# A feed-forward in two passes through DRAM, with seven block products in place of eight

## The chip, the cores and the metric

One core of one Trainium2 chip. The metric is the device time of the program in microseconds; several executions are measured, and the median is given. TensorE is PE in the profile, VectorE DVE, ScalarE ACT, GpSimd POOL, and SyncE SP; all DMAs of this kernel are issued on SP.

## The reference

Two layers of a diffusion backbone over 1280 tokens (1024 latent tokens and 256 context tokens, width 1024). Each layer has a mixer (attention, a recurrent branch, a gated MLP) and then a feed-forward with 4096 features; both end in a normalised residual sum:

```python
def _layer(x, mod, lp, ctx):
    sh1, sc1, g1, sh2, sc2, g2 = jnp.split(mod, 6, axis=-1)
    out, k, v, s = _mixer(x * (1 + sc1) + sh1, lp, ctx)
    x = _layernorm(ALPHA * x + g1 * out, lp['ln1_g'], lp['ln1_b'])
    hff = x * (1 + sc2) + sh2
    f = jnp.square(jax.nn.relu(hff @ lp['w_ff1'] + lp['b_ff1'])) @ lp['w_ff2'] + lp['b_ff2']
    x = _layernorm(ALPHA * x + g2 * f, lp['ln2_g'], lp['ln2_b'])
    return x, k, v, s
```

The change is in the line of `f`. `mod`, the modulation, is a product of a condition vector with a 1024 x 6144 matrix for each layer.

## The kernel before

**Arithmetic.** Every fp32 operand of a product is split into `hi` (12 significant bits, ACT copies it) and `lo = src - hi` (`split`, line 159; POOL or DVE subtracts, line 166). A product is then three matmuls into the same PSUM bank, hi·hi, lo·hi and hi·lo (`mm3`, lines 168 to 172). A bank holds 128 x 512, and eight banks are free in the feed-forward.

**Feed-forward.** `ff` (line 1412 on) runs over 16 chunks of 256 features. `ff1` makes a chunk's hidden features, feature-major, in three token groups A, B (512 latent tokens each) and C (256 context tokens): 8 x 3 matmuls to a bank, ACT relu (line 1386) and square (1387), and DVE squares once more in place and subtracts for the low part (1388, 1389). `ff2_mm` then makes, for each of ten blocks of 128 tokens (`BLOCKS`), 2 x 2 x 3 matmuls of 512 columns into two banks, and DVE adds them to the running sum in SBUF, `acc[t]`:

```python
nc.vector.tensor_tensor(acc[t][:, ns], b[n], (bf if c == 0 else acc[t])[:, ns], ALU.add)   # line 1446
```

So each chunk's hidden features are used at once and never leave SBUF. Weights come in pieces of 128 x 1024 (512 KB); `ahead` keeps two pieces split (`whi`, `wlo`) and four on their way (`stg`).

**The end of a layer.** Chunks 14 and 15 have their first products one after the other; then the final stage (lines 1475 to 1500) does both second products of a block in one go (24 matmuls), and the block's gate, residual and normalisation follow on DVE, with `ln_stats` (its Newton steps are lines 184 and 188). In layer 1 the last scaling is shared by POOL (line 1488, 1489) and DVE. Ahead of it, `conv` (lines 1420 to 1429) turns `acc` into `acc * gate + x` on POOL, in the background, from chunk 13's first block on.

**Order of the work.** The program is written out in one order per engine. Background streams (`add_bg`, `tick`) hand out pieces of work at a rate beside the main loops: in layer 0's feed-forward, `ada_bg` makes the remaining modulation on DVE (lines 462 to 500, rate `ABR = 0.36`), 14 halves of 16 operations. Buffers are pools: U with 30 buffers of 4 KB a partition for the whole program, X with 20 in this phase.

Of the kernel before, what the change touches and what calls it, by code (L numbers as in the profile page):

```python
# [8 lines left out]
F32 = mybir.dt.float32  # L9
# [29 lines left out]
NX = (20, 20)  # L39
# [12 lines left out]
ABR = 0.36  # L52
# [24 lines left out]
class Kern:  # L77
# [16 lines left out]
    def x_open(self, bufs):  # L94
        """the part of SBUF, and PSUM, that each phase cuts to its own sizes"""
# [62 lines left out]
    def split(self, hi, lo, src, hi_eng="act", lo_eng="pool"):  # L158
        """hi = src to 12 significant bits, lo = the rest, both exact."""
# [31 lines left out]
    def gelu2(self, dst, b):  # L191
        """dst (SBUF) = 2 gelu(b), the tanh form, of b in PSUM"""
# [23 lines left out]
    def pieces_init(self):  # L216
# [8 lines left out]
        for l in range(DEPTH):  # L225
# [26 lines left out]
    def pal(self, p, stg=False):  # L252
# [37 lines left out]
    def ahead(self, key, n_split, n_dma):  # L290
        """pieces up to n past key's are split, and n_dma past it on their way"""
        i = self.pidx[key]
        self.p_emit_split(i + 1 + n_split)
        self.p_emit_dma(i + 1 + n_dma)

# [1 line left out]
    def ada_load(self, l, part, c0, k0, alloc, s):  # L297
        """rows k0 * 128 ... and 256 columns of the modulation's weights"""
# [1307 lines left out]
```

## Time and profile before

| | |
|---|---|
| median of three runs | 3286.34 us |
| lowest, highest | 3280.35, 3291.84 us |
| span of the profiled execution | 3283.4 us |
| PE busy, matmuls and transposes | 3063.7 us, 16,368 |
| DVE busy | 2272.3 us |
| ACT busy | 1264.4 us |
| POOL busy | 1073.3 us |
| moved by DMA | 215.37 MB |

The profiled execution is one of its own; the page gives its span, from the first instruction to the last, and no other time of it. Its span lies 2.9 us below the median and within the runs shown. A matmul row's duration is longer than its share of the time, since matmuls are pipelined: the distance between two starts is what counts.

### The profile page before, as it was taken

How to read it: one execution, taken by the hardware profiler on the slowest of the kernel's cores; microseconds unless marked ns; L12 is line 12 of the kernel's file. 1: busy time of each engine (PE TensorE's matmuls, PEld its weight loads, DVE VectorE, ACT ScalarE, POOL GpSimd, SP SyncE). 2: the span in 40 equal slices, each digit the busy share in tenths (PEclk: the TensorE clock that was granted, in tenths of full speed). 3: DMA queues.
4: the chain of work that ended last, by engine and by line, in shares of the span. 5: the costliest groups of instructions: out<-in, count | busy, mean ns of one | idle time of the engine just before them, and what ended most of it. 6: DMA issues, size and time to landing. Idle time of an engine off the chain costs nothing. (4 is left out here: it accounts for less than half of the span.)

```text
span 3283.4 us, 42645 instructions
## 1 busy us (share of the span) xinstructions
PE 3063.7 (93%) x16368; PEld 2586.6 (79%) x16368; DVE 2272.3 (69%) x4688; ACT 1264.4 (39%) x2098; POOL 1073.3 (33%) x606
## 2 busy tenths in 40 slices
PE   7888999999999999999988899997899999999994
PEld 5676789777888888888877778985688888888883
DVE  8879999686767757664747999968743434343469
ACT  5444688543212121222466457872412121212121
POOL 4222245442222222226333224466411111111364
PEclk9999999999999999999999999998899999999997
DMA  6321000232222222212221100021300111111221
GB/s 223 125 83 43 15 1 14 91 109 96 91 65 90 90 78 78 90 65 90 79 76 46 55 15 1 8 103 71 116 29 36 40 38 39 39 39 39 71 90 58
DMA packets 105084, 215.37 MB, mean 66 GB/s; under 512 B 16248, under 2 KB 49800, under 8 KB 104880
## 3 DMA queue, kind: packets, MB, share of 16 engines
q1 hardware_dynamic: 104880, 212.65, 18.8%
q8 instruction: 128, 2.10, 0.3%
q14 instruction: 76, 0.62, 0.1%
HBM read 185.82 MB, written 26.81 MB: 65 GB/s over the span
## 5 line engine op out<-in xcount | busy, mean ns | idle before, releaser
L166 POOL TENSOR_TENSOR wlo<-stg,whi 128x1024 fp32r<-128x1024 f32 (+2 forms) x196 | 432.6, 2224 | 1156.3 <-ACT whi L162 967.6
L170 PE MATMUL ps<-hh,whi 128*128 128x512 f32 (+1 forms) x1808 | 647.6, 358 | 20.4 <-ACT hh L561 10.2
L172 PE MATMUL ps<-hh,wlo 128*128 128x512 f32 (+1 forms) x1808 | 645.8, 357 | 5.4 <-POOL wlo L166 5.4
L171 PE MATMUL ps<-hl,whi 128*128 128x512 f32 (+1 forms) x1808 | 643.2, 356 | 5.4 <-POOL hl L383 2.2
L1386 ACT ACTIVATE relu<-ps,pfm 128x512 f32<-128x512 f32 (+1 forms) x192 | 118.1, 616 | 1164.6 <-PE ps L172 1104.5
L1388 DVE TENSOR_TENSOR relu<-relu 128x512 f32<-128x512 f32 (+1 forms) x192 | 164.0, 855 | 489.0 <-ACT midh L1387 419.4
L1446 DVE TENSOR_TENSOR acc<-ps,acc 128x512 f32<-128x512 f32 x520 | 347.5, 687 | 207.3 <-PE ps L172 207.1
L170 PE MATMUL ps<-whi,midh 128*128 128x512 f32 x1024 | 401.1, 392 | 0.0
L172 PE MATMUL ps<-whi,midl 128*128 128x512 f32 x1024 | 400.6, 391 | 0.0
L171 PE MATMUL ps<-wlo,midh 128*128 128x512 f32 x1024 | 400.4, 391 | 0.0
L170 PEld LDWEIGHTS ps<-hh,whi 128*128 128x128 f32 x1808 | 342.8, 190 | 71.2 <-ACT hh L561 10.6
L171 PEld LDWEIGHTS ps<-hl,whi 128*128 128x128 f32 x1808 | 342.2, 189 | 61.8 <-POOL hl L383 3.9
L172 PEld LDWEIGHTS ps<-hh,wlo 128*128 128x128 f32 x1808 | 342.0, 189 | 58.8 <-POOL wlo L166 6.3
L166 POOL TENSOR_TENSOR pt<-ptf,pt 128x512 fp32r<-128x512 f32 x128 | 166.7, 1303 | 240.2 <-DVE pt L164 224.2
L1144 DVE TENSOR_SCALAR_CACHE_REDUCE S<-sc 128x512 f32<-128x512 f32 (+1 forms) x416 | 224.4, 581 | 11.2 <-PE pT L1155 9.9
L172 PEld LDWEIGHTS ps<-whi,midl 128*128 128x128 f32 x1024 | 192.9, 188 | 41.1
L170 PEld LDWEIGHTS ps<-whi,midh 128*128 128x128 f32 x1024 | 193.2, 189 | 39.7
L171 PEld LDWEIGHTS ps<-wlo,midh 128*128 128x128 f32 x1024 | 193.2, 189 | 39.5
L1147 ACT ACTIVATE S<-S,anm 128x1280 f32<-128x1280 f32 (+1 forms) x160 | 191.1, 1195 | 36.8 <-DVE anm L1146 34.5
L1155 PE MATMUL pT<-ident,S 128*128 128x128 f32 x1344 | 201.8, 273 | 2.0 <-DVE pt L1164 1.4
L162 ACT CAST whi<-stg 128x1024 fp32r<-128x1024 f32 (+2 forms) x204 | 178.2, 910 | 56.8 <-DMA stg<-in_w_ff 28.3
L1180 PE MATMUL o<-pt,vt 128*128 128x256 f32 x1024 | 190.9, 302 | 9.8 <-POOL pt L166 8.0
(318 smaller groups left out, 6133.8 us busy)
## 6 DMA issues: line engine op xcount, KB each, us to landing
stg<-in_w_ff SPq DMA_DIRECT2D x128, 512.0 KB
aslab<-in_w_ada SPq DMA_DIRECT2D x56, 512.0 KB
rx<-rx SPq DMA_DIRECT2D x40, 512.0 KB
stg<-in_w_in SPq DMA_DIRECT2D x28, 512.0 KB
araw<-in_w_ada SPq DMA_DIRECT2D x48, 256.0 KB
wada<-in_w_ada SPq DMA_DIRECT2D x16, 512.0 KB
stg<-in_w_out SPq DMA_DIRECT2D x16, 512.0 KB
yf<-ydr SPq DMA_DIRECT2D x20, 256.0 KB
```

Source lines behind the costliest of these rows:

```text
L162: nc.scalar.copy(hi, src)
L166: e.tensor_tensor(lo, src, hi.bitcast(F32), ALU.subtract)
L170: mm(out, lh, rh, start=start, stop=False)
L171: mm(out, lh, rl, start=False, stop=False)
L172: mm(out, ll, rh, start=False, stop=stop)
L1144: nc.vector.tensor_scalar(S[:, c0:c0 + n], b[:, :n], 1.0, -3.0e38, ALU.mult, ALU.max, accum_out=u["m"][:, hh, i:i + 1])
L1147: nc.scalar.activation(S[:, :c0], S[:, :c0], AF.Exp, bias=u["nm"][:, hh:hh + 1], accum_out=u["d"]["den"][:, ci % 2, hh:hh + 1])
L1155: nc.tensor.transpose(b[:, c, hh, :], u["S"][hh][:, (2 * j + c) * P:(2 * j + c + 1) * P], self.ident)
L1180: nc.tensor.matmul(o, v, pt[:, hl, c, :], start=j == 0 and c == 0 and hl == 0, stop=j == last and c == 1 and hl == 1)
L1386: nc.scalar.activation(f[:, :n], b[:, :n], AF.Relu, bias=pf[:, C_BF1 + 2 * c + m:C_BF1 + 2 * c + m + 1])
L1388: nc.vector.tensor_tensor(f[:, :n], f[:, :n], f[:, :n], ALU.mult)
L1446: nc.vector.tensor_tensor(acc[t][:, ns], b[n], (bf if c == 0 else acc[t])[:, ns], ALU.add)
```

## The change

The feed-forward makes two passes. **Pass 1** runs all 16 first products. Each feature half `m` goes to a tile `f[m]` of [128, 2, 640], in which the 1280 tokens are two halves of 640 (512 latent and 128 context tokens); ACT takes relu and square. For chunks 0 to 11 the 2 x 2 arrangement (feature half by token half) is turned into the seven left operands of a Strassen product in Winograd's form: three are the tiles themselves, four are sums on DVE, and all seven are stored to DRAM (`mc`). Chunks 12 to 15 are stored plain (`mr`). **Pass 2** (`seven`) goes through six groups `q` of two chunks. For each of seven products it loads M (`mf`, 640 KB), splits it on ACT and DVE (`mh`, `ml`), makes the weights' operand by differences on POOL (four of the seven), splits it (`wh`, `wl`), and multiplies: five token blocks of 128 x two chunks x three matmuls of 512 columns. Each result goes to one of the accumulators X1, X2, Y, Z. In the last group these are joined to the ten blocks' sums. Chunks 12 and 13 then follow as before from `mr` (`mid_load`), `conv` is added behind the first block of chunk 13 with all ten blocks, and the final stage with chunks 14 and 15 is as before. The background modulation moves from X to U and its rate from 0.36 to 0.62. X has 14 buffers and a ring of eight tiles of 5 KB (`m`), which also takes weights in the out-projection.

```diff
-NX = (20, 20)
+NX = 14
+NM = 8
+NQ = 6
-ABR = 0.36
+ABR = 0.62
...
 def ff1
+        f = [self.mt([P, 2, 640], s="f") for _ in range(2)]
...
+                nc.scalar.activation(dst, src, AF.Relu, bias=pf[:, C_BF1 + 2 * c + m:C_BF1 + 2 * c + m + 1])
                 self.tick(n / 100.0)
+            after(g)
+        for m in range(2):
+            nc.scalar.activation(f[m], f[m], AF.Square)
+        if c >= 2 * NQ:
+            for m in range(2):
+                nc.sync.dma_start(out=self.mr[l][c - 2 * NQ][:, m], in_=f[m])
+            return
+        q, k = divmod(c, 2)
+        mc = self.mc[l][q]
+        nc.sync.dma_start(out=mc[0, :, k, :], in_=f[0][:, 0, :])
+        nc.sync.dma_start(out=mc[1, :, k, :], in_=f[1][:, 0, :])
+        nc.sync.dma_start(out=mc[6, :, k, :], in_=f[1][:, 1, :])
+        s12, s34 = self.mt([P, 2, 640], s="s12"), self.mt([P, 2, 640], s="s34")
+        tt = nc.vector.tensor_tensor
+        tt(s12[:, 0], f[0][:, 1], f[1][:, 1], ALU.add)
+        tt(s12[:, 1], s12[:, 0], f[0][:, 0], ALU.subtract)
+        tt(s34[:, 0], f[0][:, 0], f[0][:, 1], ALU.subtract)
+        tt(s34[:, 1], f[1][:, 0], s12[:, 1], ALU.subtract)
+        for j, t in ((2, s12), (4, s34)):
+            nc.sync.dma_start(out=mc[j:j + 2, :, k, :].rearrange("i p n -> p i n"), in_=t)
...
+    def seven(self, l):
+        acc = {"X1": [], "X2": [], "Y": [], "Z": []}
+        where = [("Y", 0), ("X1", 0), ("Y", 1), ("X1", 1), ("X2", 1), ("Z", 0), ("X2", 0)]
...
+        def mload(n):
+            q, s = divmod(n, 7)
+            M[n] = self.mt([P, 2, 640], s="mf")
+            nc.sync.dma_start(out=M[n], in_=self.mc[l][q][s])
...
+        def prep(n):
...
+            if s == 2 and q + 1 < NQ:
+                load(q + 1)
+            if n + 1 < 7 * NQ:
+                mload(n + 1)
...
+            elif s == 2:
+                src = T[q] = self.x([P, 2, 512], s="wt")
+                tt(src, r(0, 1), r(0, 0), ALU.subtract)
...
+            wh, wl = self.u([P, 2, 512], F32R, s="wh"), self.u([P, 2, 512], F32R, s="wl")
+            self.split(wh, wl, src)
+            mh, ml = self.mt([P, 2, 640], F32R, s="mh"), self.mt([P, 2, 640], F32R, s="ml")
+            self.split(mh, ml, M.pop(n), lo_eng="dve")
...
+        def run(n):
+            q, s = divmod(n, 7)
+            mh, ml, wh, wl = W.pop(n)
+            for p in range(5):
+                b = self.ps()
+                c = slice(p * P, p * P + P)
+                for k in range(2):
+                    self.mm3(b, mh[:, k, c], ml[:, k, c], wh[:, k, :], wl[:, k, :], k == 0, k == 1)
...
+                if q:
+                    nc.vector.tensor_tensor(a, b, a, ALU.add)
...
+            if q == NQ - 1:
+                for p in range(5):
+                    join(s, p)
...
+        def join(s, p):
+            x1, x2, y = (acc[k][p] for k in ("X1", "X2", "Y"))
+            add = lambda e, a, b: e.tensor_tensor(a, a, b, ALU.add)
+            if s == 1:
+                add(nc.gpsimd, x1[:, 0], y[:, 0])
+            elif s == 3:
+                add(nc.gpsimd, x1[:, 1], y[:, 0])
+            elif s == 4:
+                add(nc.vector, x2[:, 1], x1[:, 1])
+                add(nc.gpsimd, x1[:, 1], y[:, 1])
+            elif s == 5:
+                add(nc.vector, x1[:, 1], a_of(5, p))
+            elif s == 6:
+                add(nc.vector, x2[:, 0], x2[:, 1])
+                add(nc.vector, x2[:, 1], y[:, 1])
...
 def ff
+        for c in range(NCH):
...
+            def after(g):
+                if c == NCH - 1:
+                    h2.pop(g)
+                    if g == "A":
+                        self.drain_bg()
+                        prep(0)
+                    if g == "B":
+                        prep(1)
+            self.ff1(l, c, h2, after)
+        for n in range(7 * NQ):
+            prep(n + 2)
+            if n == 7 * NQ - 2:
+                mid = self.mid_load(l, 2 * NQ, self.u)
+                self.p_emit_split(self.pidx[(l, "w2", 2 * NQ, 1)] + 1)
+            run(n)
+        acc = result()
...
-        for c in range(NCH - 2):
+        for c in range(2 * NQ, NCH - 2):
             w = [self.need((l, "w2", c, a)) for a in range(2)]
             for i, t in enumerate(BLOCKS):
...
                 if c == NCH - 3 and i == 0:
-                    self.drain_bg()
-                    self.add_bg(conv(BLOCKS[:8]), CONVR)
+                    self.add_bg(conv(BLOCKS), CONVR)
                 self.tick(2.6)
...
-        mids = [self.ff1(l, NCH - 2, h2)]
...
-                self.add_bg(conv(BLOCKS[8:]), CONVR)
-        mids.append(self.ff1(l, NCH - 1, h2, after))
         ws = [[self.need((l, "w2", c, a)) for a in range(2)] for c in (NCH - 2, NCH - 1)]
         self.drain_bg()
```

Where instructions stand now. PE's list has 360 matmul instructions fewer. On DVE, in layer 1's second pass, the order is (`ml` is M's low part, `accx` an accumulator of `seven`; a row shows what the instruction writes, reads and waits for):

```order
L168 TENSOR_TENSOR ml_26022<-mf_25964,mh_26021 128x1280 [waits DMAHW6_49,Activation_49]
L1536 TENSOR_TENSOR accx_4419_25555<-ps_26025,accx_4419_25555 128x512 [waits PE_49]
L1536 TENSOR_TENSOR accx_4421_25564<-ps_26033,accx_4421_25564 128x512 [waits PE_49]
L1536 TENSOR_TENSOR accx_4423_25573<-ps_26041,accx_4423_25573 128x512 [waits PE_49]
L1536 TENSOR_TENSOR accx_4425_25582<-ps_26049,accx_4425_25582 128x512 [waits PE_49]
L1536 TENSOR_TENSOR accx_4427_25591<-ps_26057,accx_4427_25591 128x512 [waits PE_49]
L168 TENSOR_TENSOR ml_26073<-mf_26015,mh_26072 128x1280 [waits DMAHW7_49,Activation_49]
```

Five additions from PSUM and one splitting of 1280 columns repeat for each product; before, a chunk had twenty such additions (line 1446) in one piece and twelve operations for the hidden features (1388, 1389) ahead of them.

On SP, in the same pass, the loads of M (`mf`, line 1471) and the weights' pieces for chunks 12 on (`stg`) stand in one queue:

```order
L1471 DMA mf_27205<-mc_5_119 128x1280 [waits DMAHW7_49,DVE_49]
L1471 DMA mf_27255<-mc_5_119 128x1280 [waits DMAHW1_49,DVE_49]
L260 DMA stg_27783<-in_w_ff 128x1024 [waits DMAHW4_49,Pool_49]
L1471 DMA mf_27305<-mc_5_119 128x1280 [waits DMAHW2_49,DVE_49]
L1471 DMA mf_27357<-mc_5_119 128x1280 [waits DMAHW6_49,DMAHW3_49,DVE_49]
L260 DMA stg_27789<-in_w_ff 128x1024 [waits DMAHW4_49,Pool_49]
```

Each load of M waits for DVE, which reads the tile that is to be overwritten.

On POOL, at the end of layer 1 before, `conv` (lines 1426 and 1428) follows the weights of chunk 14:

```order
L166 TENSOR_TENSOR wlo_27565<-stg_27366,whi_27564 128x1024 [waits PE_49,DMAHW0_49,Activation_49,Pool_49]
L166 TENSOR_TENSOR wlo_27569<-stg_27368,whi_27568 128x1024 [waits PE_49,DMAHW1_49,Activation_49,Pool_49]
L1426 TENSOR_TENSOR acc_22737<-acc_22737,g2b_27507 128x1024 [waits DMAHW2_49,DVE_49]
L1428 TENSOR_TENSOR acc_22737<-acc_22737,rx_27509 128x1024 [waits DMAHW3_49,Pool_49]
L1426 TENSOR_TENSOR acc_22754<-acc_22754,g2b_27507 128x1024 [waits DVE_49]
L1428 TENSOR_TENSOR acc_22754<-acc_22754,rx_27545 128x1024 [waits DMAHW4_49,Pool_49]
L1426 TENSOR_TENSOR acc_22771<-acc_22771,g2b_27507 128x1024 [waits DVE_49]
L1428 TENSOR_TENSOR acc_22771<-acc_22771,rx_27609 128x1024 [waits DMAHW7_49,Pool_49]
```

Now, behind the weights of chunks 14 and 15 (`conv` is lines 1612 and 1614, the final stage's scaling 1665):

```order
L168 TENSOR_TENSOR wlo_28036<-stg_28033,whi_28035 128x1024 [waits DMAHW1_49,PE_49,Activation_49]
L168 TENSOR_TENSOR wlo_27955<-stg_27952,whi_27954 128x1024 [waits DMAHW2_49,PE_49,Activation_49]
L1612 TENSOR_TENSOR accx_4419_25555<-accx_4419_25555,g2b_27907 128x1024 [waits DVE_49]
L1614 TENSOR_TENSOR accx_4419_25555<-accx_4419_25555,rx_27909 128x1024 [waits DMAHW3_49,Pool_49]
L1612 TENSOR_TENSOR accx_4421_25564<-accx_4421_25564,g2b_27907 128x1024 [waits DVE_49]
L1614 TENSOR_TENSOR accx_4421_25564<-accx_4421_25564,rx_27974 128x1024 [waits DMAHW6_49,Pool_49]
L1612 TENSOR_TENSOR accx_4423_25573<-accx_4423_25573,g2b_27907 128x1024 [waits DVE_49]
...
L1612 TENSOR_TENSOR accx_4462_25748<-accx_4462_25748,g2b_28143 128x1024 [waits DVE_49]
L1614 TENSOR_TENSOR accx_4423_25573<-accx_4423_25573,rx_28055 128x1024 [waits DMAHW2_49,Pool_49]
L1614 TENSOR_TENSOR accx_4425_25582<-accx_4425_25582,rx_28107 128x1024 [waits DMAHW3_49,Pool_49]
...
L1614 TENSOR_TENSOR accx_4462_25748<-accx_4462_25748,rx_28149 128x1024 [waits DMAHW1_49,Pool_49]
L1665 TENSOR_TENSOR accx_4419_25555<-accx_4419_25555,ag_28153 128x960 [waits Activation_49]
```

All ten products with the gate stand ahead of the last eight additions, and all 20 operations of `conv` between the last of four weights' splits and the first scaling; no first product lies beside it any more.

## Rows read from the trace of the kernel before

**Rows 1.** Span of the core and its mean granted TensorE clock
```profile
core 0: 3283.4 us, clock 0.974
```

**Rows 2.** Page, part 1: busy time, share and instructions of each engine
```profile
PE 3063.7 (93%) x16368; PEld 2586.6 (79%) x16368; DVE 2272.3 (69%) x4688; ACT 1264.4 (39%) x2098; POOL 1073.3 (33%) x606
```

**Rows 3.** Windows: each engine's busy time, granted clock, DMA share, GB/s
```profile
core 0: us, PE busy (x) PEld busy (x) DVE busy (x) ACT busy (x) POOL busy (x), PEclk, DMA share, GB/s
0.00:100.00 100.00, 72.58 (x384) 51.09 (x385) 78.73 (x146) 52.77 (x72) 38.11 (x30) 0.91 0.62 206
900.00:1000.00 100.00, 100.00 (x464) 82.54 (x463) 69.22 (x96) 19.06 (x27) 25.02 (x10) 1.00 0.26 81
2600.00:2700.00 100.00, 100.00 (x479) 84.07 (x478) 45.24 (x62) 19.06 (x28) 20.02 (x8) 1.00 0.12 43
3181.00:3283.00 102.00, 54.42 (x237) 43.98 (x235) 94.53 (x184) 12.92 (x12) 47.03 (x22) 0.78 0.13 52
```

**Rows 4.** Timeline of ACT (start, duration, idle before): first relu of two chunks
```profile
2746.26 0.69 ACT L1386 ACTIVATE relu<-ps,pfm 128x512 f32<-128x512 f32 x1 [31.81 <-PE ps L172]
...
2801.13 0.69 ACT L1386 ACTIVATE relu<-ps,pfm 128x512 f32<-128x512 f32 x1 [31.82 <-PE ps L172]
```

**Rows 5.** Timeline of PE, line 170: every third matmul of 512 columns
```profile
2499.97 0.39 PE L170 MATMUL ps<-whi,midh 128*128 128x512 f32 x1
...
2510.17 0.39 PE L170 MATMUL ps<-whi,midh 128*128 128x512 f32 x1
```

**Rows 6.** Groups of DVE by shape, layer 0's feed-forward (count, busy, mean ns, idle)
```profile
L1446 DVE TENSOR_TENSOR acc<-ps,acc 128x512 f32<-128x512 f32 x252 | 166.9, 685 | 67.7 <-PE ps L172 67.5
L479 DVE SCALAR_TENSOR_TENSOR aacc<-aslab,scond,aacc 128x512 f32<-128x512 f32 x196 | 165.0, 877 | 4.7 <-DMA aslab<-in_w_ada 4.7
L1388 DVE TENSOR_TENSOR relu<-relu 128x512 f32<-128x512 f32 x52 | 47.1, 906 | 133.6 <-ACT midh L1387 133.6
```

**Rows 7.** Groups of DVE by shape, layer 1's feed-forward
```profile
L1389 DVE TENSOR_TENSOR midc<-relu,midc 128x256 fp32r<-128x256 f32 x26 | 36.0, 1386 | 0.9
L1389 DVE TENSOR_TENSOR midl<-relu,midh 128x512 fp32r<-128x512 f32 x52 | 36.0, 692 | 2.7
```

**Rows 8.** Groups of POOL by shape, layer 1's feed-forward
```profile
L166 POOL TENSOR_TENSOR wlo<-stg,whi 128x1024 fp32r<-128x1024 f32 x52 | 130.0, 2521 | 579.6 <-ACT whi L162 413.9 <-DVE midc L1389 165.7
```

**Rows 9.** Groups of ACT by shape, layer 0's feed-forward
```profile
L162 ACT CAST whi<-stg 128x1024 fp32r<-128x1024 f32 x52 | 52.4, 1041 | 0.0
L1386 ACT ACTIVATE relu<-ps,pfm 128x512 f32<-128x512 f32 x52 | 35.8, 688 | 434.3 <-PE ps L172 434.3
```

**Rows 10.** Chain of waits of 2190 to 2370 us: start, us, DMA
```profile
2195.13 10.99 DMA ag<-in_ln_g
...
2365.25 5.58 DMA stg<-in_w_ff
```

**Rows 11.** Timeline of DVE in layer 1's final stage
```profile
3199.95 0.22 DVE L184 SCALAR_TENSOR_TENSOR rst<-rsy,bv 128x1 f32<-128x1 f32 x1
...
3205.41 2.23 DVE L184 SCALAR_TENSOR_TENSOR rst<-rsy,bv 128x1 f32<-128x1 f32 x1
...
3211.31 1.21 DVE L1481 TENSOR_TENSOR acc<-acc,fb 128x1024 f32<-128x1024 f32 x1
...
3220.69 1.21 DVE L1481 TENSOR_TENSOR acc<-acc,fb 128x1024 f32<-128x1024 f32 x1
```

**Rows 12.** Timeline of POOL: first and last of layer 1's conv, first scaling
```profile
3104.34 2.41 POOL L1426 TENSOR_TENSOR acc<-acc,g2b 128x1024 f32<-128x1024 f32 x1
...
3182.54 2.47 POOL L1428 TENSOR_TENSOR acc<-acc,rx 128x1024 f32<-128x1024 f32 x1
...
3205.29 2.32 POOL L1488 TENSOR_TENSOR acc<-acc,ag 128x960 f32<-128x960 f32 x1 [6.14 <-ACT acc L1484]
```

**Rows 13.** Timeline of DVE in layer 0's final stage
```profile
1607.71 1.23 DVE L1481 TENSOR_TENSOR acc<-acc,fb 128x1024 f32<-128x1024 f32 x1
...
1613.34 1.23 DVE L1481 TENSOR_TENSOR acc<-acc,fb 128x1024 f32<-128x1024 f32 x1
```

More of the change, by code (lines that the diff above doesn't have):

```diff
@@ L257, in pal @@
             return self.lx
+        if ph == "out" and self.phase == "out" and not stg:
+            return self.mt
         return self.x if ph == self.phase and self.X is not None else self.u
@@ L288, in need, with ahead @@
         return p[3], p[4]
[L290 to L294, printed above, removed]
+    def ahead(self, key, n_split, n_dma, last):
+        i, m = self.pidx[key], self.pidx[last]
+        self.p_emit_split(min(i + n_split, m) + 1)
+        self.p_emit_dma(min(i + n_dma, m) + 1)
     def ada_load(self, l, part, c0, k0, alloc, s):
@@ L480, in ada_bg @@
                         yield 0.6
-                hi, lo = (self.x([P, 2, 512], F32R, s="aspl") for _ in range(2))
+                hi, lo = (self.u([P, 2, 512], F32R, s="aspl") for _ in range(2))
                 self.split(hi, lo, acc)
@@ L628, in cst_load @@
         self.rx1 = [self.DR.tile([10, P, D], F32, name=f"rx1_{l}") for l in range(DEPTH)]
+        self.mc = [[self.DR.tile([7, P, 2, 640], F32, name=f"mc{l}_{q}") for q in range(NQ)] for l in range(DEPTH)]
+        self.mr = [[self.DR.tile([P, 2, 2, 640], F32, name=f"mr{l}_{c}") for c in range(NCH - 2 * NQ)] for l in range(DEPTH)]
         self.xn2 = self.DR.tile([10, P, D], F32, name="xn2")
@@ L1363, in out_proj, with mt, ff1 @@
         return h2
-    def ff1(self, l, c, h2, after=None):
+    def mt(self, shape, dt=F32, s="m"):
+        return self.X.tile(list(shape), dt, tag="m", name=self.nm(s), bufs=NM)
+    def ff1(self, l, c, h2, after):
         nc = self.nc
         w = [self.need((l, "w1", c, a)) for a in range(2)]
-        mid = {}
         pf = self.pfm[l]
+        f = [self.mt([P, 2, 640], s="f") for _ in range(2)]
         for g in "ABC":
@@ new lines, in ff1, with mid_load @@
+        s12, s34 = self.mt([P, 2, 640], s="s12"), self.mt([P, 2, 640], s="s34")
[6 more added lines that the diff above has]
+            nc.sync.dma_start(out=mc[j:j + 2, :, k, :].rearrange("i p n -> p i n"), in_=t)
+    def mid_load(self, l, c, alloc):
+        nc = self.nc
+        src = self.mr[l][c - 2 * NQ]
+        mid = {}
+        for g in "ABC":
+            st = self.x([P, 2, GN[g]], s="mst")
@@ L1391, in ff1 @@
-            if after is not None:
-                after(g)
+                nc.sync.dma_start(out=st, in_=src[:, :, "AB".index(g), 0:512])
+                mid[g] = (alloc([P, 2, 512], F32R, s="midh"), alloc([P, 2, 512], F32R, s="midl"))
+            self.split(*mid[g], st, lo_eng="dve")
         return mid
@@ L1414, in ff @@
         self.psn = 8
-        bf = self.bc_row(I["b_ff2"][l:l + 1], "bf2")
-        acc = {}
-        gb = {}
+        prep, run, result = self.seven(l)
+        for c in range(NCH):
+            if l == 0 and c == 1:
+                self.add_bg(itertools.chain(self.ada_bg(0, (5,)), self.ada_bg(1, (0, 1, 2, 3, 4, 5))), ABR)
+            def after(g):
[7 more added lines that the diff above has]
+            self.ff1(l, c, h2, after)
+        gb = {}
+        for n in range(7 * NQ):
[5 more added lines that the diff above has]
+        acc = result()
         def conv(ts):
@@ L1429, in conv @@
                 del x
                 yield 2.3
-        for c in range(NCH - 2):
-            if l == 0 and c == 1:
-                bf = None
-                self.add_bg(itertools.chain(self.ada_bg(0, (5,)), self.ada_bg(1, (0, 1, 2, 3, 4, 5))), ABR)
-            mid = self.ff1(l, c, h2)
+        mids = []
+        for c in range(2 * NQ, NCH - 2):
             w = [self.need((l, "w2", c, a)) for a in range(2)]
             for i, t in enumerate(BLOCKS):
-                if i == 4:
-                    self.ahead((l, "w2", c, 1), 2, 4)
+                if c < NCH - 3 and i == 4:
+                    nxt = self.mid_load(l, c + 1, self.u)
+                    self.p_emit_split(self.pidx[(l, "w2", c + 1, 1)] + 1)
+                if c == NCH - 3 and i in (2, 5):
+                    j = len(mids)
+                    mids.append(self.mid_load(l, NCH - 2 + j, self.x if j else lambda sh, dt, s: self.mt(sh, dt, s)))
+                    self.p_emit_split(self.pidx[(l, "w2", NCH - 2 + j, 1)] + 1)
```

132 lines of the change are left out of this document (95 added, 37 removed).

## Prediction

> **What bounds the kernel now.** I read the span first, then the page's busy shares, then windows laid over single stages, because a share over the whole span averages stages with different limits. The span of the profiled execution is 3283.4 us [rows 1]; the median of the runs shown is 3286.34, so I make the sum against 3283.4 and add 2.9 at the end. TensorE is busy 93% of the span, VectorE 69%, GpSimd 33% [rows 2]. The windows say where this average is true: in the feed-forward of both layers PE is busy 100 of 100 us at a granted clock of 1.00, with DVE at 69 (layer 0, where the background modulation runs on it) and 45 (layer 1); in the last 102 us it is the reverse, DVE 94.5 of 102 and PE 54 [rows 3]. So in the feed-forward a matmul less is worth its full pitch, as long as nobody else becomes late, and in the final stage DVE's time counts and PE's does not. The last thing to look at is a wait that no engine's share shows: in the final stage one tiny DVE instruction, 0.22 us when it is undisturbed, takes 2.23 us, and it started 0.12 us after a GpSimd operation of 2.32 us over SBUF [rows 11, 12].
>
> **What a matmul is worth.** Line 170 issues every third matmul; from the first to the last row shown are 15 such steps, 45 matmuls, in 10.20 us, that is 0.2267 us each [rows 5]. A chunk is 54.87 us from one first relu to the next [rows 4]; its second product has 10 blocks x 12 matmuls = 120 x 0.2267 = 27.2 us, so the first product has 27.7.
>
> **Removed.** For 3072 of 4096 features, eight block products become seven: 6 groups x one block product of 5 x 6 = 30 matmuls = 180 a layer, 360 in all, at 0.2267 us: **-81.6 us**. The order of PE's instructions has these 360 fewer, so that the change doesn't do what it says is excluded. A block product now takes 30 x 0.2267 = 6.80 us, and each layer has 42 of them; that is the cover under which everything added in the second pass must fit.
>
> **Pass 1, 27.7 us of PE a chunk.** DVE loses the two operations per relu tile and gets four sums of 640. Two-input operations from SBUF cost 0.69 us at 512 columns and 1.21 at 1024 [rows 7, 11], so 0.82 at 640, four of them 3.3; by the longer mean of 0.906 at 512 [rows 6] they are 4.5. In layer 0 the modulation is squeezed from 54.87 us chunks into these: 16 operations and a little per chunk at 0.877 [rows 6], 14 to 15.5 us. Together about 20 of 27.7: it fits. ACT has six relus and two squares, about 10 us, and the whi copies at 1.04 [rows 9]. Stores (2.3 MB a chunk for the seven combinations) plus loads come to some 5.5 MB in 27.7 us, 200 GB/s; the opening of the program moves 206 GB/s at a DMA share of 0.62 [rows 3]. Hidden, cost 0. Without that cover, a DVE that is late by 1 us a chunk would cost 16 us a layer.
>
> **Pass 2, steady.** Per product DVE has five additions from PSUM at 0.687 [rows 6] and one `ml` of 1280 columns with two SBUF inputs: 0.69 at 512 and 1.21 at 1024 make 1.47 at 1280. Sum 4.9 of 6.80. GpSimd has 1 `wl` of 1024 per product and four differences per seven products, 11 x 2.5 [rows 8] = 27.5 of 47.6 us per group. When `ml` comes up GpSimd is in the middle of an operation with chance 0.58, for 1.25 us on average: expected wait 0.7 us, DVE at 5.6 of 6.80. ACT has the copies of W and M, 1.04 + 1.3. DMA carries 0.95 MB a product, 140 GB/s. Cost 0; PSUM's eight banks cover single late additions (five banks are one product).
> The Trainium skill, page "SBUF — State Buffer", section "Who interferes with whom", says that a VectorE instruction with two SBUF inputs and a GpSimd instruction that reads SBUF exclude each other for their whole length, the first to start winning, and that one SBUF input at most does not contend. By that rule each `ml` can lose a whole GpSimd operation and the additions from PSUM none; the trace agrees (0.22 to 2.23 us), and if every `ml` lost one the sum would be the second rival's.
>
> **Between the passes.** M 0 must be stored, loaded, split. The nearest rows are a load of 5.58 us, or at worst 10.99, in other places [rows 10]; the first chunks were stored long ago, but W's differences, `h2` and the m buffers that the last chunk frees stand in the way. I take 1.5 us a layer, near the short end since the first two products are prepared during the last chunk of the first product; bounds 0 and 12. **+3.**
>
> **End of pass 2.** In the last group the joins come on top: 20 DVE operations of 512 with two SBUF inputs at 0.69 = 14 us, 15 on GpSimd, and the first `mid` tiles of chunk 12 (a splitting of 2560 columns, 3 us on DVE). DVE's load in the last four products is about 4 x 4.9 + 14 + 3 = 37 us, plus port waits, against 27 of PE; the eight banks and the following chunk, where DVE has only 14 of 27 us to do, take most of it. I take 4 us a layer; bounds 0 (banks cover it) and 12 (the excess of 10 and a wait). **+8.**
>
> **The conversion in the tail.** This is the term that I hold to be the largest. `acc * gate + x`, 20 GpSimd operations at 2.4 us, today runs from 3104 to 3185 us [rows 12], under the two first products of chunks 14 and 15, which keep PE 55 us. After the change nothing but chunk 13's second product (27.2 us) lies between its start and the final stage, and four `wlo` go ahead of it: 4 x 2.5 + 20 x 2.4 = 58 us, 24 operations, of which about 11 or 12 fit. Some 12 run into the final stage; PE needs 5.4 us for its first block, so about 10 meet DVE. What a GpSimd operation costs DVE there is read from the pitch of line 1481: 9.37 us per block in layer 1, with two GpSimd scalings per block [rows 11], 5.63 in layer 0, with none [rows 13]; (9.37 - 5.63) / 2 = 1.9 us. So 10 x 1.9 = 19 us a layer; bounds 0 (all hidden) and 20 x 1.9 = 38. Late next is the scaling at line 1665, which queues behind the eight last additions on GpSimd, but it has a pitch of 9.4 us and 4.6 to do, and catches up. The loads of x (512 KB each) wait for slots of chunk 13's weights; at 5.58 us, several in flight, they keep the additions' pace. **+38.**
>
> **Out-projection and start.** Other slots for its weights; the nearest wait is the load of 10.99 us there [rows 10]. Taken as 0, bounds -11 and +11.
>
> **Sum.** -81.6 + 3 + 8 + 38 = -32.6; 3283.4 - 32.6 = 3250.8; with the 2.9 to the median **3254 us**.
>
> **The rivals.**
> *The conversion is hidden* (the loads come early, GpSimd ends near the end of chunk 13, or DVE's waits overlap PE's): the term of 38 falls away, 3254 - 38 = 3216. For it: the four `wlo` could run ahead of chunk 13, and DVE spends part of the final stage waiting anyway. Against it: even the 20 operations alone are 48 us in 27.
> *DVE becomes the bound of pass 2.* If each `ml` loses a whole GpSimd operation, DVE needs 4.9 + 2.5 = 7.4 us per product instead of 6.80: 84 x 0.6 = +50, 3304. It decides from a mean wait of 1.9 us; for it: the copies on ACT release `wl` and `ml` close together, so that they start in step, and `midc` shows it, 1.386 us on average for 256 columns where 512 take 0.692 [rows 7]. Against it: GpSimd is idle for 42% of a group, and the other `midl` rows, 0.692 us on average, lost nothing [rows 7].
> *The M loads become the bound, the other side.* M has two buffers in flight in the m pool: a load starts when DVE has split the M before last (about 4 us after its product's start, with the copy and the queue), so two products can't be shorter than the landing time L plus 4 us. It decides from L = 2 x 6.80 - 4 = 9.6 us. With 5.58 [rows 10] it never binds; with 10.99 [rows 10] a product takes 7.5, and 84 x 0.7 = +58: 3312, **slower** than before. For it: loads of W (2 MB per group) and of the next pieces stand in the same queue. Against it: 140 GB/s is less than the opening's 206.
> **How the numbers follow.** Forecast 0.60, hidden conversion 0.16, DVE bound 0.12, M loads 0.07, other 0.05. The forecast's own range is 3225 to 3285: its terms' bounds do not all fall on one side. No change means within 0.3% of the median, 3276.5 to 3296.2, about what a measurement of this kernel can tell. Faster: 0.57 + 0.16 + 0.02 = 0.75. Same: 0.03 of the forecast, 0.04 of the DVE bound (half its waits), 0.01 other = 0.08. Slower: 0.08 + 0.07 + 0.02 = 0.17. The range reaches down past the hidden conversion, to 3208, and up to the middle of the DVE bound, 3306.
>
> **What would show it.** Windows over pass 2 should have PE at 100%, pitch of product 6.8 us, DVE 75 to 85%. DVE idle behind PE there means the steady term is right; PE waiting for `ml` means the second rival, for `mf` the third. In the final stage GpSimd rows of lines 1612 and 1614 beside long `rst` rows show the tail term: 20 us each layer from the end of chunk 13 to the span's end more than today. A pitch of more than 27.7 us in pass 1, or PE idle between the passes by more than 12 us, would make the prediction wrong.

## The result and the profile after

| | before | after |
|---|---|---|
| median of the runs | 3287.93 us (3280.35 to 3291.84) | 3240.86 us (3239.53 to 3242.14) |
| ratio to before | | 0.986, 95% interval 0.9843 to 0.9877 |
| span of the profiled execution | 3283.4 us | 3237.4 us |

The change is faster by 47.1 us; 32 were forecast (3254). The two spans differ by 46.0 us, so the traces can be compared. Span, busy shares and four windows of the changed kernel (us, busy time of PE, PEld, DVE, ACT, POOL, granted clock, DMA share, GB/s), which answer to [rows 1 to 3]:

```profile
core 0: 3237.4 us, clock 0.970
```
```profile
PE 2996.8 (93%) x16008; PEld 2524.8 (78%) x16008; DVE 2201.4 (68%) x4458; ACT 1416.6 (44%) x2144; POOL 1374.1 (42%) x722
```
```profile
900.00:1000.00 100.00, 100.00 (x509) 83.66 (x508) 64.62 (x85) 31.27 (x38) 28.90 (x11) 1.00 0.62 206
2600.00:2700.00 100.00, 100.00 (x535) 85.95 (x535) 11.27 (x12) 32.20 (x39) 21.74 (x9) 1.00 0.36 125
2860.00:3000.00 140.00, 140.00 (x613) 114.88 (x612) 107.78 (x125) 47.36 (x43) 92.83 (x34) 1.00 0.43 136
3123.00:3237.00 114.00, 55.95 (x230) 44.08 (x228) 89.02 (x182) 12.42 (x10) 68.82 (x31) 0.76 0.21 78
```

The first two windows lie in pass 1 of layers 0 and 1, the third in pass 2: PE is busy throughout at a clock of 1.00, as it was before. In pass 2 DVE has risen to 77% and GpSimd to 66%, and PE waits for neither. The last window is layer 1's final stage, where DVE and not PE decides.

Where the 46 us come from is read between markers that both traces have (each is the start or end of a row of the trace; the differences are mine):

| stretch | before | after | difference |
|---|---|---|---|
| start to the end of chunk 0's first product, layer 0 | 790.0 | 784.5 | -5.4 |
| from there to PE's first matmul of the final stage, layer 0 | 804.6 | 772.5 | -32.1 |
| from there to the first gated product (`fb`) on DVE | 6.1 | 21.0 | +14.9 |
| from there to the last sum of the final stage | 61.5 | 61.3 | -0.2 |
| mixer of layer 1, to the end of chunk 0's first product | 726.2 | 726.0 | -0.2 |
| to PE's first matmul of the final stage, layer 1 | 791.6 | 755.2 | -36.4 |
| to the first `fb` | 6.1 | 21.0 | +14.9 |
| to the end | 97.4 | 96.0 | -1.4 |

PE's first matmul of the final stage stands in these rows, of the kernel before (layers 0 and 1) and of the changed one, where the last of chunk 13's matmuls, with `midc`, ends the feed-forward:

```profile
1594.52 0.39 PE L170 MATMUL ps<-whi,midh 128*128 128x512 f32 x1
...
3179.94 0.39 PE L170 MATMUL ps<-whi,midh 128*128 128x512 f32 x1
```
```profile
1557.00 0.39 PE L172 MATMUL ps<-whi,midh 128*128 128x512 f32 x1
...
3120.40 0.40 PE L172 MATMUL ps<-whi,midh 128*128 128x512 f32 x1
```

The feed-forwards gain 68.5 of the 81.6 us that the removed matmuls are worth. The first `fb` then comes 14.9 us later after PE's start than before, in each final stage, and that takes back 30.

The wait stands in three rows of DVE, layer 1 (start, duration, idle before and releaser):

```profile
3122.47 1.27 DVE L1631 TENSOR_TENSOR accx<-ps,accx 128x512 f32<-128x512 f32 x2
3141.36 1.29 DVE L1657 TENSOR_TENSOR fb<-ps,g2b 128x512 f32<-128x512 f32 x2 [17.61 <-POOL accx L1614]
...
3144.33 5.16 DVE L1658 TENSOR_TENSOR accx<-accx,fb 128x1024 f32<-128x1024 f32 x1
```

DVE has finished chunk 13 and then is idle for 17.6 us, until an addition of the conversion (line 1614) has finished; the first sum of the stage (line 1658) then takes 5.16 us. GpSimd in the same stretch, where `x8` is eight operations in a row:

```profile
3112.53 17.01 POOL L1612 TENSOR_TENSOR accx<-accx,g2b 128x1024 f32<-128x1024 f32 x7 [2.36 <-DVE accx L1631]
3129.49 18.91 POOL L1614 TENSOR_TENSOR accx<-accx,rx 128x1024 f32<-128x1024 f32 x8
3160.00 2.27 POOL L1665 TENSOR_TENSOR accx<-accx,ag 128x960 f32<-128x960 f32 x1 [11.59 <-ACT accx L1661]
```

The ten products with the gate end at 3129.5, the eight last additions at 3148.4, while the last addition from PSUM of chunk 13 ended at 3123.7. In the instructions' order `fb` waits for an X buffer, which a tile of the residual `x` holds until its addition is done. Twelve of the conversion's operations (four products, eight additions) are left when PE begins the stage at 3120.4, and eleven when DVE has ended chunk 13; 12 were forecast.

In layer 0 PE has to wait as well. From its first matmul of the stage to the end of the stage's last sum (the changed kernel, then the kernel before):

```profile
1557.00:1640.39 83.39, 65.21 (x305) 53.46 (x303) 59.86 (x168) 36.07 (x63) 31.82 (x14) 0.90 0.32 113
```
```profile
1594.52:1663.29 68.77, 65.78 (x321) 54.61 (x320) 64.86 (x171) 40.54 (x73) 9.77 (x4) 1.00 0.20 77
```

PE is idle for 18 us of this stretch, where it was idle for 3, and its granted clock is 0.90 where it was 1.00. From 1587 to 1597 us it is 0.50, the lower of its two levels (1.2 GHz); in the 10 us before PE was busy for 2.3. What the clock costs here was not told apart.

### The profile page after: what moved, and what is told of

Read it like the earlier page. It is cut to its first block, busy times and chain, and to the rows that moved or that the text cites. A ratio compares the mean times of both kernels' runs of the same rounds, so it can differ in the third digit from the quotient of the medians.

```text
span 3237.4 us, 42444 instructions
## 1 busy us (share of the span) xinstructions
PE 2996.8 (93%) x16008; PEld 2524.8 (78%) x16008; DVE 2201.4 (68%) x4458; ACT 1416.6 (44%) x2144; POOL 1374.1 (42%) x722
## 5 line engine op out<-in xcount | busy, mean ns | idle before, releaser
L168 POOL TENSOR_TENSOR wlo<-stg,whi 128x1024 fp32r<-128x1024 f32 (+2 forms) x148 | 305.1, 2072 | 705.4 <-ACT whi L164 697.4
L1387 ACT ACTIVATE f<-ps,pfm 128x512 f32<-128x512 f32 (+1 forms) x192 | 118.2, 616 | 484.5 <-PE ps L174 476.2
L173 PE MATMUL ps<-wl,mh 128*128 128x512 f32 x840 | 329.6, 392 | 0.0
L172 PE MATMUL ps<-wh,mh 128*128 128x512 f32 x840 | 328.0, 390 | 1.4 <-DVE accy L1536 1.4
L174 PE MATMUL ps<-wh,ml 128*128 128x512 f32 x840 | 328.8, 391 | 0.0
L168 DVE TENSOR_TENSOR ml<-mf,mh 128x1280 fp32r<-128x1280 f32 x84 | 173.4, 2064 | 222.2 <-ACT mh L164 189.6
L164 ACT CAST mh<-mf 128x1280 fp32r<-128x1280 f32 x84 | 106.3, 1266 | 271.0 <-PE ps L173 215.6
L168 POOL TENSOR_TENSOR wl<-wraw,wh 128x1024 fp32r<-128x1024 f32 x60 | 170.1, 2844 | 111.8 <-ACT wh L164 111.8
L164 ACT CAST whi<-stg 128x1024 fp32r<-128x1024 f32 (+2 forms) x156 | 133.3, 875 | 164.7 <-PE ps L173 65.6
L172 PEld LDWEIGHTS ps<-wh,mh 128*128 128x128 f32 x840 | 157.7, 188 | 37.7 <-DVE accy L1536 2.3
```

Source lines behind the costliest of these rows:

```text
L164: nc.scalar.copy(hi, src)
L168: e.tensor_tensor(lo, src, hi.bitcast(F32), ALU.subtract)
L172: mm(out, lh, rh, start=start, stop=False)
L173: mm(out, lh, rl, start=False, stop=False)
L174: mm(out, ll, rh, start=False, stop=stop)
L1387: nc.scalar.activation(dst, src, AF.Relu, bias=pf[:, C_BF1 + 2 * c + m:C_BF1 + 2 * c + m + 1])
```

## The experiments

Times are medians; the changed kernel has 3240.86. The kernel before was measured beside each (3287.7 to 3288.7).

**1. The conversion left out.**

```diff
-                x = self.x(s="rx")
-                a = acc[t].rearrange("p d n -> p (d n)")
-                nc.sync.dma_start(out=x, in_=self.rx1[l][t])
-                nc.gpsimd.tensor_tensor(a, a, gb[strm(t)], ALU.mult)
-                yield 2.3
-                nc.gpsimd.tensor_tensor(a, a, x, ALU.add)
-                del x
                 yield 2.3
```

> Leaves out acc*gate + x ahead of the last two chunks (both operations on GpSimd and the loads of x), so it shows the whole cost of that conversion. In the changed kernel the first addition of the final stage starts 18 to 19 us after the last one of chunk 13, where PE needs 5.4 us. Theory A (the conversion makes DVE wait at the head of the final stage, 13.5 us a layer): that distance falls to 6 us, and the time by 25 to 30 us against the changed kernel, to about 3214. Theory B (the recorded step: leftover GpSimd operations lengthen DVE's own, 1.9 us each, all through the stage): the distance stays and the pitch of the stage shortens. Theory C (the head waits for the weights or hidden features of chunks 14 and 15): no change.

3217.64 us (ratio 0.9786, 0.9767 to 0.9805), 23 less than the changed kernel. The first `fb` comes 5.2 us after the last addition:

```profile
3109.72 1.28 DVE L1624 TENSOR_TENSOR accx<-ps,accx 128x512 f32<-128x512 f32 x2
3114.91 1.38 DVE L1650 TENSOR_TENSOR fb<-ps,g2b 128x512 f32<-128x512 f32 x2 [3.91 <-PE ps L174]
```

So the conversion costs 23 us, and C falls. The distance falls as A says, and from the first `fb` to the end layer 1 takes 97.6 us against 96.0, no shorter, which speaks against B. But the run takes away the wait and all of GpSimd's operations together, so it can't say alone which of them costs the time.

**2 to 4. Other buffers for `fb`, for `x`, for both.**

```diff
-            f = self.x(s="fb")
+            f = self.u(s="fb")
```

> Only the buffer of fb (the gated product in the final stage) moves from X to U, where buffers are free. Theory A in its narrow form (fb waits for an X buffer that a conversion's addition gives back): the first fb starts 6 us after chunk 13's last addition, and DVE then waits for the third block's conversion instead; a gain of 3 to 10 us a layer, 6 to 20 in all. Theory B: the same number of GpSimd operations meets DVE, 0.

3241.0 us (ratio 0.9861, 0.9839 to 0.9882): no gain. And yet the wait is gone. DVE of this run, layer 1:

```profile
3122.13 1.28 DVE L1631 TENSOR_TENSOR accx<-ps,accx 128x512 f32<-128x512 f32 x2
3125.09 1.38 DVE L1657 TENSOR_TENSOR fb<-ps,g2b 128x512 f32<-128x512 f32 x2 [1.68 <-PE ps L174]
...
3130.22 2.32 DVE L186 SCALAR_TENSOR_TENSOR rst<-rsy,bv 128x1 f32<-128x1 f32 x1
3132.58 2.31 DVE L190 SCALAR_TENSOR_TENSOR rsy<-rst,rsy 128x1 f32<-128x1 f32 x1
3134.93 2.33 DVE L186 SCALAR_TENSOR_TENSOR rst<-rsy,bv 128x1 f32<-128x1 f32 x1
3137.29 2.32 DVE L190 SCALAR_TENSOR_TENSOR rsy<-rst,rsy 128x1 f32<-128x1 f32 x1
3139.65 2.32 DVE L186 SCALAR_TENSOR_TENSOR rst<-rsy,bv 128x1 f32<-128x1 f32 x1
```

and GpSimd beside it:

```profile
3130.14 16.52 POOL L1614 TENSOR_TENSOR accx<-accx,rx 128x1024 f32<-128x1024 f32 x7
```

The first `fb` starts 16 us earlier than in the changed kernel, and then the Newton steps, operations on one column that take 0.16 to 0.22 us by themselves, take 2.32 us each, in step with GpSimd's additions of 2.4 us: one step is held up per addition. From PE's first matmul of the stage to the end (the changed kernel, then this run):

```profile
3120.40:3237.40 117.00, 58.55 (x241) 46.22 (x239) 91.62 (x183) 12.42 (x10) 71.42 (x32) 0.77 0.22 81
```
```profile
3120.06:3238.90 118.84, 61.18 (x241) 47.85 (x239) 109.08 (x183) 12.41 (x10) 71.82 (x32) 0.77 0.22 80
```

DVE is busy for 91.6 of 117.0 us in the changed kernel and for 109.1 of 118.8 here. The time that the wait cost comes back as longer instructions. A in its narrow form is wrong: the buffer decides where the time is lost, not whether.

```diff
-                x = self.x(s="rx")
+                x = self.u(s="rx")
```

> Only the buffers of the residual x that the conversion adds move from X to U, so that their loads need not wait for buffers of chunk 13's weights and features. The conversion's order on GpSimd becomes gate, add, gate, add by blocks instead of ten gates and then eight additions. Theory A (order and buffers): the first blocks are ready before the final stage, no buffer of X is held by a waiting x, first fb 6 us after chunk 13's last addition, gain 8 to 13 us a layer, to about 3215 to 3225. Theory B (number of GpSimd operations beside DVE): 0.

3250.21 us (ratio 0.9886, 0.9868 to 0.9904): 9 slower, where 16 to 26 less were expected. The order of the conversion became gate, add by blocks as intended, and the first `fb` came early, but twelve operations instead of eleven were left, and layer 1's stage took 3.0 us longer (120.0 from PE's first matmul of the stage to the end, against 117.0). The other 5 to 6 us were lost in layer 1's mixer, whose first relu came at 2331.3 in place of 2325.6 although layer 0 had ended at the same time. Why the mixer took longer was not tried; its granted clock was 0.95 against 0.96.

> Both buffers in U. Theory A: as the run with x alone, at most 3 us better, since x in U frees X for fb already. If the order of the conversion mattered and not the buffers, this equals the run with x alone exactly; if only fb's buffer mattered, it equals the run with fb alone.

3242.07 us, with runs from 3237.9 to 3251.83: too scattered to tell the two effects apart. It is no better than the changed kernel, which speaks against A again.

This left a theory D: on SBUF, DVE's operations with two inputs there and GpSimd's operations exclude each other, so that GpSimd's leftover costs the stage its time in one form or the other. If so, it is GpSimd's work in the stage that must go.

**5. The eighth product's time put back.**

```diff
+            if s == 6:
+                for p in range(5):
+                    b = self.ps()
+                    c = slice(p * P, p * P + P)
+                    for k in range(2):
+                        self.mm3(b, mh[:, k, c], ml[:, k, c], wh[:, k, :], wl[:, k, :], k == 0, k == 1)
```

> Puts the eighth block product's time back on PE alone: behind every seventh product its 30 matmuls are done once more into banks that nobody reads. Theory A (the second pass is bound by PE, a matmul is worth its pitch of 0.2267 us): 12 x 6.80 = +81.6 us against the changed kernel, to about 3322; the repeats also give DVE and GpSimd 6.8 us per group, so 75 to 82. Rival (the second pass is bound by DVE and GpSimd, which share work on SBUF): well under 40.

3313.33 us (ratio 1.0072, 1.0053 to 1.0091): 72.5 more than the changed kernel. From the end of chunk 0's first product to PE's first matmul of the final stage it takes 39.1 us longer in layer 0 (811.6 against 772.5) and 41.5 in layer 1 (796.7 against 755.2), 80.6 of the 81.6 put in. PE binds pass 2. That the whole time grows by less lies outside this stretch: layer 1's stage is 2.8 us shorter (114.2 against 117.0), and the parts ahead of chunk 0 and behind layer 0's stage are 3 us shorter; why was not tried. With eight products' time on PE the two passes are slower than the kernel before by 0.7%: what they add costs 25 us.

**6. `ml` done twice.**

```diff
-            self.split(mh, ml, M.pop(n), lo_eng="dve")
+            mf = M.pop(n)
+            self.split(mh, ml, mf, lo_eng="dve")
+            nc.vector.tensor_tensor(ml, mf, mh.bitcast(F32), ALU.subtract)
```

> Every ml of the second pass (1280 columns, two SBUF inputs on DVE) is done twice, 84 more operations. In the changed kernel ml took 2.06 us on average (1.47 was estimated for one that waits for nothing), five additions 0.683 each: DVE 5.5 of 6.80 us per product. Theory A (1.3 us of slack are left): the second costs 1.5 to 2.1, so DVE needs 7.0 to 7.5 and the time grows by 84 x 0.2 to 0.7 = 15 to 60 us. Rival 1 (DVE has much more room, waits were in its slack): 0 to 10. Rival 2 (DVE bounds the pass already): 84 x 1.5 = +126 or more.

3315.8 us (ratio 1.0082, 1.0065 to 1.0099): 75 more, above the 60 that I gave theory A and far below rival 2. The groups of DVE in pass 2 of the changed kernel (count, busy us, mean ns, idle before):

```profile
L168 DVE TENSOR_TENSOR ml<-mf,mh 128x1280 fp32r<-128x1280 f32 x21 | 41.3, 1968 | 7.9 <-ACT mh L164 7.9
L1536 DVE TENSOR_TENSOR accx<-ps,accx 128x512 f32<-128x512 f32 x59 | 39.1, 686 | 16.4 <-PE ps L174 16.1
```

and of this run, in the same 140 us, with the window's own row:

```profile
L168 DVE TENSOR_TENSOR ml<-mf,mh 128x1280 fp32r<-128x1280 f32 x18 | 42.7, 2373 | 9.3 <-ACT mh L164 9.3
L1513 DVE TENSOR_TENSOR ml<-mf,mh 128x1280 fp32r<-128x1280 f32 x17 | 41.9, 2462 | 0.0
L1538 DVE TENSOR_TENSOR accx<-ps,accx 128x512 f32<-128x512 f32 x45 | 28.4, 677 | 0.0
```
```profile
2860.00:3000.00 140.00, 126.08 (x508) 97.21 (x507) 130.69 (x120) 40.11 (x37) 104.78 (x35) 0.95 0.37 124
```

The additions from PSUM stay at 0.68 us in both, and their idle time falls to nothing; only `ml` grows, to 2.37 and 2.46 us. DVE is busy for 130.7 of the 140 us, and PE, which was busy for all of them, for 126.1, at a granted clock of 0.95 in place of 1.00. In the changed kernel DVE needs 1.97 + 5 x 0.685 = 5.4 us of a product's 6.80; 1.4 us are its whole slack, and a second `ml`, with what GpSimd takes from it, is more than that. DVE did not bind, but was the next to.

**7 and 8. The conversion of the last five, or seven, blocks on DVE.** The list of blocks for `conv` is cut, and in the final stage the others go another way:

```diff
-                    self.add_bg(conv(BLOCKS), CONVR)
+                    self.add_bg(conv(BLOCKS[:5]), CONVR)
...
+        for t in BLOCKS[5:]:
+            late_x(t)
...
+            if t in late:
+                x = late.pop(t)
+                for n in range(2):
+                    ns = slice(n * 512, n * 512 + 512)
+                    nc.vector.tensor_tensor(r[:, ns], b[n], r[:, ns], ALU.add)
+                nc.vector.tensor_tensor(r, r, gb[strm(t)], ALU.mult)
+                nc.vector.tensor_tensor(r, r, x, ALU.add)
...
```

(`late_x` loads x, and the context's gate, to U.)

> The conversion on GpSimd is kept for the first five blocks only, which fit beside chunk 13. For the other five DVE adds the product to acc from PSUM, then multiplies by the gate and adds x (two operations of 1024 in place of one, +1.22 us a block); their x lies in U, loaded ahead of the last features. Theory D (in the final stage DVE's operations on SBUF and GpSimd's exclude each other, so that each of the 11 leftover GpSimd operations costs DVE's stage 1.2 to 1.9 us whether as a wait ahead of it or as longer operations in it): 10 of them go, 12 to 19 us, for 6.1 us of DVE: 6 to 13 us a layer, 12 to 26 in all, to 3215 to 3229. Rival (the cost of the conversion is the wait for its results): DVE has 6 us a layer more to do and the first blocks are as late as before: +0 to +12.

3215.05 us (ratio 0.978, 0.9762 to 0.9798), 26 less than the changed kernel: the upper end of what D gave, and level with the run without any conversion (3217.64; the intervals overlap). DVE does more and the stage is shorter: from PE's first matmul of the stage to the end 103.2 us in layer 1, against 117.0.

> As the run with five blocks, with three on GpSimd and seven on DVE (+8.5 us of DVE a layer). Theory D: nothing more is won by taking GpSimd's operations away once none is left in the final stage, so 0 to 6 us slower than the run with five. Rival: if each GpSimd operation costs wherever it runs, faster than with five by up to 4 us.

3216.81 us (ratio 0.9778, 0.9761 to 0.9796), the same as with five, as D says. The rival's 4 us lie within the interval, about 6 us to either side, so the run doesn't exclude it.

**9 and 10. The last scaling on DVE alone**, by itself and with the five blocks.

```diff
-                for e, c in ((nc.gpsimd, slice(0, lc)), (nc.vector, slice(lc, D))):
-                    e.tensor_tensor(r[:, c], r[:, c], ag[:, c], ALU.mult)
-                    e.tensor_tensor(r[:, c], r[:, c], ab_[:, c], ALU.add)
+                nc.vector.tensor_tensor(r, r, ag, ALU.mult)
+                nc.vector.tensor_tensor(r, r, ab_, ALU.add)
```

> Only the last scaling of layer 1's final stage (ag, ab) goes from GpSimd and DVE together to DVE alone: 20 GpSimd operations of up to 2.3 us go, DVE's two pieces of 64 columns become two of 1024. DVE gets 2 x (1.21 - 0.2) = 2.0 us a block more. Theory D (each GpSimd operation costs DVE 1.9 us here): 20 x 1.9 - 10 x 2.0 = 18 us less, 10 to 18 with what other waits take back; to about 3223 to 3231 from 3240.9. Rival (GpSimd's scaling runs beside DVE's work and costs it nothing): 20 us more, to 3261.

> The conversion of five blocks on GpSimd, and the last scaling on DVE alone: no GpSimd operation is left in layer 1's final stage but the tail of the five blocks' conversion. Theory D: the stage is ten blocks of about 5.6 + 1.2 / 2 + 2.0 = 8.2 us of DVE, 82 in place of 94 with the five blocks alone; 10 to 15 us less than that run's 3215.05, to 3200 to 3205. Rival (the gain of the five-block run came from waits at the head of the stage only): +10 to +20, to 3225 to 3235.

3222.84 us (ratio 0.9802, 0.9785 to 0.9818) and 3201.06 us (ratio 0.9734, 0.9715 to 0.9754): 18.0 and 39.8 less than the changed kernel, the first at the upper end of what D gave and the second inside it. The Newton step of layer 1's stage, with GpSimd's scaling beside it (the run without the conversion), with the conversion too (the run with `fb` in U), and without the scaling (run 10):

```profile
L186 DVE SCALAR_TENSOR_TENSOR rst<-rsy,bv 128x1 f32<-128x1 f32 x30 | 34.6, 1153 | 0.5
```
```profile
L186 DVE SCALAR_TENSOR_TENSOR rst<-rsy,bv 128x1 f32<-128x1 f32 x30 | 40.8, 1359 | 0.5
```
```profile
L186 DVE SCALAR_TENSOR_TENSOR rst<-rsy,bv 128x1 f32<-128x1 f32 x30 | 6.3, 211 | 0.2
```

30 instructions on one column go from 34.6 us to 6.3 when GpSimd has no scaling there. It is not always the Newton step that is held up. In the changed kernel itself, with scaling and conversion, it takes 16.6 us, and other operations of DVE with two inputs in SBUF are the longer ones, above all the sums:

```profile
L186 DVE SCALAR_TENSOR_TENSOR rst<-rsy,bv 128x1 f32<-128x1 f32 x30 | 16.6, 559 | 0.2
L1658 DVE TENSOR_TENSOR accx<-accx,fb 128x1024 f32<-128x1024 f32 x10 | 20.0, 2003 | 0.0
```

In the run without the conversion the ten sums take 12.2 us. DVE's operations with one input in SBUF don't change: the 20 of `fb` (the other input lies in PSUM) take 13.4 us in the changed kernel and 13.5 in the runs without the conversion and with `fb` in U, and the 20 of `bst`, the sums for the normalisation (line 207), 13.4 and 13.5. The kernel of run 10 is the fastest of the study, 2.7% below the kernel before.

**11. The same scaling in the kernel before.** The edit is that of run 9.

> The kernel before, with only the last scaling of layer 1 on DVE alone. It tells whether what that move won on the changed kernel belongs to the change. Theory D (each GpSimd operation in the final stage costs DVE 1.9 us, in either kernel): 10 to 18 us less, 3270 to 3277. Rival (only the changed kernel's stage, with its leftover conversion, is so crowded): 0 or slower.

3263.47 us (ratio 0.9926, 0.9909 to 0.9942): 24 less, more than the 10 to 18 that D gave here. Layer 1's stage, from PE's first matmul to the end, takes 80.3 us against 103.5, 23.2 less. The profiled spans differ by 17 alone (3266.5), since in this execution layer 1's mixer, whose instructions are the same, took 6 us longer. That gain is not the change's; it was there to be had before.

## Why the prediction was right, and where its sizes were off

The time lies inside the range, and the mechanism held in the main: 360 matmuls at their pitch, DVE, GpSimd and the loads of pass 2 beneath PE, a part given back in the tails. The range was 98 us wide, more than the removed matmuls are worth, so that to land in it says little by itself. Against the profiled spans the sum was -32.6 and -46.0 was measured. By its terms:

- **Removed matmuls, -81.6.** Right: PE is busy for 100 of 100 us in the windows of pass 1 and 140 of 140 in that of pass 2, and putting the time back moved the final stages by 80.6 us.
- **Pass 1, 0.** Right as a sum: the first products of chunks 1 to 15 take 426.5 us in layer 0 (784.5 to 1211.06) and 407.7 in layer 1 (2365.2 to 2772.94), 834.3 together; before, it was 804.6 + 791.6 less 28 second products of 27.2 us, 834.6. The layers differ. A chunk takes 27.27 us in layer 1 (409.06 us for 15, between the relu rows below), 27.7 had been taken. In layer 0 it takes 28.51, so 18.6 us more in all; before, layer 0 took 12.9 us longer than layer 1 from chunk 1's first relu to the last relu (776.5 against 763.6). The 14 halves of the modulation thus cost 6 us more than they did; PE waited for them only once, 2.0 us, and the reason for the rest was not tried. By the prediction's own sign, a pitch of more than 27.7 us, layer 0 of pass 1 fails; 12.9 of its 18.6 us stood there before as well.

```profile
2364.74 0.46 ACT L1387 ACTIVATE f<-ps,pfm 128x256 f32<-128x256 f32 x1
...
2773.80 0.47 ACT L1387 ACTIVATE f<-ps,pfm 128x256 f32<-128x256 f32 x1
```

- **Pass 2, 0.** For DVE right: it was forecast at 5.6 of 6.80 us, 5.4 was measured; a wait of 0.7 us for `ml` had been expected, and 1.97 - 1.47 = 0.5 was found in the window (the shortest `ml` takes 1.47 us, the mean of all 84 is 2.06). For PE not quite. The rows are its first matmul of pass 2 and of chunk 12, in layers 0 and 1:

```profile
1211.06 0.40 PE L172 MATMUL ps<-wh,mh 128*128 128x512 f32 x1
...
1500.47 0.39 PE L172 MATMUL ps<-whi,midh 128*128 128x512 f32 x1
```
```profile
2772.94 0.39 PE L172 MATMUL ps<-wh,mh 128*128 128x512 f32 x1
...
3062.36 0.39 PE L172 MATMUL ps<-whi,midh 128*128 128x512 f32 x1
```

  42 products take 289.4 us, 6.89 each in place of 6.80: 7.6 us in both layers, where 0 stood. PE waited for 0.7 us a layer of it, for an addition; the rest is 0.229 us a matmul in place of the 0.2267 of [rows 5], and its cause is open.
- **Between the passes, +3.** Nothing: in both layers the first matmul of pass 2 starts 0.12 us after the last one of pass 1.
- **End of pass 2, +8.** Chunks 12 and 13 take 56.5 us in layer 0 and 58.0 in layer 1 (from the rows above to PE's first matmul of the final stage), where 240 matmuls need 54.4: 5.7. PE's waits there are 0.3 and 1.8 us, for additions of line 1631.

  The feed-forwards thus lose 13.1 of the 81.6 us, and 0 + 3 + 8 = 11 had been forecast. That the sum comes near is luck: more than half of the loss lies in the steady pass, which was put at nothing.
- **The conversion, +38.** This is the step that failed in its size: +14.9 - 0.2 + 14.9 - 1.4 = +28 by the table, and 23 by the run that leaves it out. The 5 between are in the stretch from PE's start of layer 0's stage to the end of chunk 0's first product in layer 1. It takes 793.8 us in the kernel before, 799.5 in the run without the conversion, and 799.9 in run 11, which has the instructions of the kernel before up to there; so the 5 are no more than two executions differ by. The count was right (12 operations run into the stage); the price of 1.9 us for each of the 10 that meet DVE was not, it is 23 / 20 = 1.15. The 1.9 came from the stage's pairs of scalings [rows 11, 13], and for them it holds: by run 9 it is (18.0 + 20) / 20 = 1.9. Why an operation in the dense row costs less is argued and not shown: DVE's operations with one input in SBUF go on beside it, and 5 us of the row lie under PE's first block, in which DVE has nothing to do. The form was another, too: a wait for a buffer, which the forecast didn't have, and not longer operations. Run 2 showed that the two are worth the same here, 3241.0 and 3240.86; nothing in the forecast said so.
- **Out-projection and start, 0 between -11 and 11.** -5.4 in layer 0 and -0.2 in layer 1. Chunk 0's first product of layer 0 ends at 790.0 and 790.1 in the two profiles without the change and between 779.1 and 787.6 in those with it, so the gain is the change's and its size uncertain by some 4 us; what of it is the other buffers was not tried.

Together -81.6 + 13.1 + 28.2 - 5.6 = -45.9.

The rivals: the hidden conversion did not come (it cost 23 of the 38). DVE did not bind pass 2; it was 1.4 us a product short of it, and run 6 showed what follows beyond. M's loads did not bind: PE stood at 140 of 140 us in the window of pass 2, with 136 GB/s moved, where 140 had been estimated.

The Trainium skill, page "SBUF — State Buffer", section "Who interferes with whom", says that a VectorE instruction with two SBUF inputs contends with a GpSimd instruction that reads SBUF, and that one with at most one SBUF input, outside the modes that use both of VectorE's ports, does not. The runs agree with both halves: DVE's operations with two SBUF inputs lose up to a whole GpSimd operation (2.32 us in place of 0.2), and the additions with one input in PSUM lose nothing (0.67 to 0.69 us each in pass 2, in every run).

## What to carry to other kernels

GpSimd's operations and those of DVE that read two inputs from SBUF are one resource where both stand in the same stage: count their times together, and don't hand work to GpSimd because it looks idle. A wait that is taken away there may come back as longer instructions, so look at the sum of DVE's busy and idle time in the stage before and after. And an expensive operation that was hidden under other work must keep its cover when a change reorders that work: here 48 us of GpSimd lost the cover of 55 us of first products, and took back 23 of the 82 us.

## What was not expected of the hardware

That an instruction on one column of 128 partitions takes 2.2 us beside GpSimd stood in one row of before [rows 11]. That five of them follow each other at 2.32 us, in step with GpSimd, was new. So was what it is worth: moving the 20 scalings of GpSimd (43 us of its time) to DVE makes a stage that is bound by DVE 18 us shorter, and 23 in the kernel before. It follows from what the rows show: such an instruction is held up for up to a whole GpSimd operation of 2.3 us, ten times its own time, while DVE does the same scaling in 1.21 us.
